# Two weight sums per block pair, and the residual additions of two down-projection parts, moved from VectorE to GpSimd

## The chip, the cores and the metric

The program runs on one core of a Trainium2 chip. The core has a matrix engine (PE, TensorE), two elementwise engines that matter here (DVE, VectorE, and ACT, ScalarE), a programmable engine (POOL, GpSimd) and a queue engine (SP, SyncE) that issues DMA transfers. Each engine takes its instructions strictly in the order in which the built program lists them, and engines wait for one another by semaphores. POOL issues DMA transfers too: those that add into what already lies in on-chip memory (accumulating DMAs). The metric is the device time of one execution in microseconds (us); lower is better.

## The reference

The model is a trunk of two layers on 512 tokens of width 1024 in float32. Each layer mixes tokens by three gated branches, multiplies the merged result by `w_o` and adds it to `x`, then does a gated feed-forward step (the part that is changed), then a gated per-layer embedding:

```python
x = x + merged @ w_o[i]
h = rmsnorm(x, norm_ffn[i])
x = x + (jax.nn.silu(h @ w_ffn_gate[i]) * (h @ w_ffn_up[i])) @ w_ffn_down[i]
h = rmsnorm(x, norm_ple[i])
x = x + jax.nn.sigmoid(h @ w_ple_gate[i]) * (p[i] @ w_ple_in[i])
```

The feed-forward width is 2816, that is 22 blocks of 128.

## The kernel before, in words

Activations are held transposed: 8 chunks of 128 features by 512 tokens, `x[0]` to `x[7]`. A float32 operand is split into a high part in the matrix engine's reduced type (ACT, line 147) and the rest, the low part (DVE, line 161), and a product is three matrix products: high by high, high by low, low by high.

**The output projection** (`w_o`, L930) makes one chunk m at a time: its weights are loaded by SP (L175) and split, PE multiplies, DVE adds the result to the old `x[m]` (loaded by SP at L938), and ACT and DVE split the scaled sum into the halves `wo_h`. `quarters` (L958) makes, after every second chunk, four sums of halves of tokens and chunks (`wo_t`) and splits them (`wo_rp`, `wo_v`, `wo_b`, `wo_z`); the feed-forward step multiplies by these.

**The feed-forward step** (`ffn`, L1100) goes over three parts of 8, 7 and 7 pairs; a pair, counted 0 to 21 here, is gate block `fb` with up block `fb`. `seven` (L989) computes a pair by seven products in place of eight (a two by two scheme over gate and up, halves of the weights' rows, and halves of the tokens). For that it needs four sums of weight halves. The first two, s1 and s2, are made by DMA: SP loads a half (L999, L1000), POOL issues a DMA that adds another half onto it (L1004). The third and fourth are `s3 = s1 + a22` and `s4 = s3 + g[:, up]`, where `a22` is a separate load (tile `ffn_r`, L1002) and `g` holds the gate weights (tile `ffn_wr`, L1001). All of `g`, `a22`, (s1, s2) and (s3, s4) are then split by ACT and DVE; the split of (s3, s4) goes to the tiles `ffn_pt` for even pairs and `ffn_y` for odd ones.

The sums lie in four wide slots: three that rotate for (s1, s2) and a single one for (s3, s4), so the third sum of a pair can only be written once the split of the pair before has read the slot. `ffn_qk_4772` names the tile of the first two slots in layer one, `ffn_qk_4773` that of the third slot and of (s3, s4). There are two buffers of `ffn_r` and three of `ffn_wr`, which the weights of `w_o` and of the down projection share.

After each part, 8 chunks of the down projection are made (L1121 to L1129): PE multiplies, DVE scales the result by the row factor into `ffn_t`, and adds it onto `x[m]`. After the third part the sum is also scaled and split for the next step.

**What sets the order.** PE's instructions stand as written, which the program asks for explicitly. Those of the other engines are put in order by a scheduler that works through them by priority, its own estimate of their lengths, and their dependencies; the weight work of `seven` has a raised priority (L993). `behind` (L1081) adds an order that is not a dependency: in the kernel before it holds s3 of a pair behind the low part of `a22`, and, for all of the first part and the first pairs of the others, behind a marked point of the work ahead (`self.mark` is the low half of chunk 4 in `w_o`).

Of the kernel before, what the change touches and what calls it, by code (L numbers as in the profile page):

```python
# [12 lines left out]
F32R = mybir.dt.float32r  # L13
I32 = mybir.dt.int32
AF = mybir.ActivationFunctionType
ALU = mybir.AluOpType
# [4 lines left out]
P = 128  # L21
# [18 lines left out]
PARTS = (range(0, 8), range(8, 15), range(15, 22))  # L40
# [25 lines left out]
class Net:  # L66
# [922 lines left out]
    def seven(self, wg, wu, bs, tags, spare, md, first, fb):  # L989


        nc = self.nc
        with self.tc.high_priority(offset=min(self.w_ahead, self.tc.cur_priority - self.p0)):  # L993
            lo, up = slice(0, 512), slice(512, 1024)
            g, a22 = self.sb("wr", [P, 1024]), self.sb("r", [P, 512])
            sums = self.sums[self.sevens % 3], self.sums[3]
            self.sevens += 1
            s1, s2, s3, s4 = (s[:, q:q + 512] for s in sums for q in (0, 512))
            nc.sync.dma_start(s1, wg[:, lo])  # L999
            nc.sync.dma_start(s2, wu[:, up])  # L1000
            nc.sync.dma_start(g, wg)  # L1001
            nc.sync.dma_start(a22, wu[:, up])  # L1002
            for q in (s1, s2):
                nc.gpsimd.dma_start(q, wu[:, lo], accum_op=ALU.add)  # L1004
            ws = {}

            def halve(hi, lo, src, names):
                i = self.split(hi, lo, src)
                for q, name in enumerate(names):
                    c = slice(q * 512, q * 512 + 512)  # L1010
                    ws[name] = (hi[:, c], lo[:, c])
                return i

            wide = lambda: (self.sb("wh", [P, 1024], F32R), self.sb("wl", [P, 1024], F32R))
            i = halve(*wide(), g, ("a11", "a12"))
            if fb == 1:
                self.behind(i, self.held)
            low = halve(self.sb("kh", [P, 512], F32R), self.sb("a", [P, 512], F32R), a22, ("a22",))
            halve(*wide(), sums[0], ("s1", "s2"))
            i = self.tt(s3, s1, a22, ALU.add)  # L1020
            self.behind(i, low)
            if first or fb < 3:
                self.behind(i, self.held if fb else self.mark)
            self.tt(s4, s3, g[:, up], ALU.add)
            halve(*spare, sums[1], ("s3", "s4"))
        A, C, Q = (self.ps(t, (P, 2, 256)) for t in tags)

        def product(out, w, b, first):
            wh, wl = ws[w]
            mm = nc.tensor.matmul  # L1030
            for k in range(4):
                c = slice(k * P, k * P + P)
                bh, bl = bs[k][b]
                mm(out, wh[:, c], bh, start=first and k == 0, stop=False, skip_group_check=True)  # L1034
                mm(out, wh[:, c], bl, start=False, stop=False, skip_group_check=True)  # L1035
                mm(out, wl[:, c], bh, start=False, stop=k == 3, skip_group_check=True)  # L1036
            self.chunk2()

        o = self.sb("t", [P, 2, 256])
        p1, p4 = o[:, 0], o[:, 1]  # L1040
        p5 = self.sb("a", [P, 256])
        gg, uu = self.sb("t", [P, 2, 256]), self.sb("t", [P, 2, 256])
        head = fb == 0
        product(A[:, 0], "a11", "b11", True)
        self.act(p1, A[:, 0], AF.Copy)
        if head:
            product(Q[:, 1], "a12", "b21", True)
            product(C[:, 0], "s4", "b22", True)
        product(Q[:, 0], "a22", "t4", True)
        self.act(p4, Q[:, 0], AF.Copy)  # L1050
        five = C[:, int(head)]
        product(five, "s2", "t1", True)
        self.flush(self.act(p5, five, AF.Copy))
        if not head:
            product(A[:, 0], "a12", "b21", False)
        product(Q[:, 0], "s1", "t3", False)
        product(A[:, 1], "s3", "t2", True)
        if head:
            self.tt(gg[:, 0], Q[:, 1], p1, ALU.add)
            self.tt(gg[:, 1], C[:, 0], p5, ALU.add)  # L1060
        else:
            product(C[:, 0], "s4", "b22", False)
        rb = self.rb.rearrange("p (a b) -> p a b", a=2)
        self.tt(p5, p4, p5, ALU.subtract)
        self.tt(gg[:, 0], gg[:, 0] if head else A[:, 0], rb[:, 0], ALU.mult)
        self.tt(p1, A[:, 1], p1, ALU.subtract)
        self.tt(uu[:, 0], p1, Q[:, 0], ALU.subtract)
        self.tt(uu[:, 1], uu[:, 0], p5, ALU.add)
        self.tt(gg[:, 1], gg[:, 1] if head else C[:, 0], p1, ALU.subtract)
        self.tt(gg[:, 1], gg[:, 1], rb[:, 1], ALU.mult)  # L1070

        def rest(then):
            i = self.act(gg, gg, AF.Silu, table="silu")
            if then is not None:
                self.behind(i, then)
            self.tt(gg, gg, uu, ALU.mult)
            self.held = self.split(*self.halves(md), gg.rearrange("p a b -> p (a b)"))

        self.pending.append(rest)
# [19 lines left out]

    def ffn(self, h, x):  # L1100
        self.phase = "ffn"
        i = self.i
        self.halfs, self.pending = 0, []
        st, hn, bs = [], [], self.four
        spare = [[self.sb(t, [P, 1024], F32R) for _ in range(2)] for t in ("pt", "y")]
        md8 = [self.sb(t, [P, 2, 512], F32R) for t in ["v"] * 3 + ["z"] + ["y"] * 3]
        md8.append(tuple(self.sb("e", [P, 512], F32R) for _ in range(2)))
        self.sums, self.sevens = [t for _ in range(2) for t in self.parts_of("qk", [1024], 2)], 0
        for part in PARTS:
            mids = []  # L1110
            for f, fb in enumerate(part):
                tags = (("mm", "mm", "mm"), ("sc", "sc", "av"))[fb % 2]
                md = md8[f]
                mids.append(md)
                wg, wu = self.a["w_fg"][i, fb], self.a["w_fu"][i, fb]
                self.seven(wg, wu, bs, tags, spare[fb % 2], md, part[0] and f < 2, fb)
            self.flush()
            down = [self.a["w_fd"][i, m][:, part[0] * P:(part[-1] + 1) * P] for m in range(KD)]
            two = [self.ps(("mm", "sc")[fb % 2 == 0]) for _ in range(2)]
            self.pair(two, down[:2], mids)  # L1120
            for m in range(KD):  # L1121
                if m < 2:
                    ps = two[m]
                else:
                    ps = self.ps("mm")
                    self.gemm(ps, down[m], mids)
                d = self.sb("t", [P, 512])
                self.tt(d, ps, self.rb, ALU.mult)
                self.tt(x[m], x[m], d, ALU.add)  # L1129
                if part is PARTS[-1]:  # L1130
                    if m in (0, 2):
                        qk = self.parts_of("qk", [2, 512], 2, F32R)
                    hn.append(self.norm_chunk(m, x[m], self.par(i, "ple", m),
                                              qk[m % 2] if m < 4 else "z", st))
        self.main_norm(st[0])
        return hn
# [347 lines left out]
```

## Time and profile before

| What | Value |
|---|---|
| median of 2 runs | 1769.13 us (1768.71 to 1769.55) |
| span of the profiled execution, first to last instruction | 1766.6 us |
| median less span | 2.5 us |
| PE busy | 1759.3 us |
| DVE busy | 1408.6 us |
| ACT busy | 885.5 us |
| POOL busy (DMA issue included) | 98.4 us |

The profiled execution has no separate device time; its span lies 2.5 us below the median of the runs, and sums below are made against the span. Busy time is the union of an engine's instructions; PE's are pipelined and overlap, so that a stream of matrix products counts as busy throughout. The granted clock of PE was 1.000 over the whole span. In layer one, `w_o` runs from about 445 to 489 us and the feed-forward step from 491.6 to about 840 us; in layer two the step begins at 1366.7 us.

### The profile page before, as it was taken

Reading aid. Unit: us, or ns where it says so; the run is one execution under the profiler, and the core shown is the slowest. Engines: PE = TensorE matmul, PEld = TensorE weight load, DVE = VectorE, ACT = ScalarE, POOL = GpSimd, SP = SyncE. Lnnn points to the kernel's source line nnn. Section 1 sums busy time; section 2 is a strip of 40 time slices with the busy share of each in tenths; the row PEclk is TensorE's granted clock in tenths of the full one; section 3 lists DMA queues with packets and bytes.
Section 4 is the critical chain, followed back from the end, with each engine's and each line's share of the span. In section 5 each row is a group of like instructions: output and inputs, shape, how many; then the busy total and the mean of one; then the engine's idle time right before and its main releaser. Section 6 shows DMA issues by size and latency. Waiting matters only on the chain.

```text
span 1766.6 us, 27127 instructions
## 1 busy us (share of the span) xinstructions
PE 1759.3 (100%) x10146; PEld 1551.8 (88%) x10146; DVE 1408.6 (80%) x2354; ACT 885.5 (50%) x1529; POOL 98.4 (6%) x114
## 2 busy tenths in 40 slices
PE   9999999999999999999999999999999999999998
PEld 7888888888899899998888888888888998989987
DVE  7967988998898587787777688889887976867776
ACT  5576555325565254454545655552356643534444
POOL 0000000000111010100000000000001110101000
PEclk9999999999999999999999999999999999999999
DMA  6575641334757365544446655322356674655332
GB/s 231 158 186 160 162 123 54 102 100 150 222 153 196 106 173 156 137 126 127 151 137 173 180 148 154 108 73 94 101 183 194 168 179 118 172 141 156 99 104 96
DMA packets 112548, 253.95 MB, mean 144 GB/s; under 512 B 14368, under 2 KB 23328, under 8 KB 112416
## 3 DMA queue, kind: packets, MB, share of 16 engines
q1 hardware_dynamic: 99024, 227.83, 42.0%
q0 software_dynamic: 12672, 23.07, 8.1%
q8 instruction: 80, 1.31, 0.3%
q10 hardware_dynamic: 720, 1.31, 0.2%
q14 instruction: 52, 0.43, 0.1%
HBM read 214.41 MB, written 7.34 MB: 126 GB/s over the span
## 4 chain that ended last, share of the span: by engine, by line
PE 92%; DVE 4%; DMA 2%; ACT 2%; issue 1%; SPq 0%; POOL 0%; ACTq 0%; POOLq 0%; DVEq 0%
PE ffn_mm L1034 4%; PE ffn_mm L1036 4%; PE ffn_mm L182 4%; PE ffn_mm L181 4%; PE ffn_mm L183 4%; PE ffn_mm L1035 4%; PE ffn_sc L1036 3%; PE ffn_sc L1034 3%; PE ffn_sc L1035 3%; PE mergea_mm L182 2%; PE mergea_mm L183 2%; PE mergea_mm L181 2%; PE gateb_mm L182 2%; PE gateb_mm L183 2%; PE gateb_mm L181 2%; PE wo_mm L182 2%
## 5 line engine op out<-in xcount | busy, mean ns | idle before, releaser
L164 DVE SCALAR_TENSOR_TENSOR conv_z<-glu_z,pre_par,conv_z 128x512 f32<-128x512 f32 x240 | 179.6, 748 | 3.5
L147 ACT ACTIVATE ffn_wh<-ffn_wr 128x1024 fp32r<-128x1024 f32 (+1 forms) x92 | 92.8, 1015 | 111.9 <-PE ffn_mm L182 81.4
L1004 POOL DMA_DIRECT2D ffn_qk<-w_fu x88 | 78.1, 978 | 605.6 <-DMA ffn_qk<-w_fu 289.7
L161 DVE TENSOR_TENSOR ffn_wl<-ffn_wr,ffn_wh 128x1024 fp32r<-128x1024 f32 (+1 forms) x92 | 107.4, 1173 | 5.3 <-ACT ffn_wh L147 4.6
L161 DVE TENSOR_TENSOR ffn_t<-ffn_mm,wo_rb 128x512 f32<-128x512 f32 (+1 forms) x64 | 38.7, 605 | 68.4 <-PE ffn_mm L183 68.4
L147 ACT ACTIVATE mergea_wh<-mergea_wr 128x1024 fp32r<-128x1024 f32 (+1 forms) x32 | 27.1, 848 | 96.8 <-PE mergea_mm L182 79.5
L147 ACT ACTIVATE ffn_wh<-ffn_qk 128x1024 fp32r<-128x1024 f32 x44 | 46.7, 1061 | 37.1 <-PE ffn_mm L182 15.9
L161 DVE TENSOR_TENSOR ffn_wl<-ffn_qk,ffn_wh 128x1024 fp32r<-128x1024 f32 x44 | 53.9, 1224 | 10.7 <-ACT ffn_wh L147 10.7
L161 DVE TENSOR_TENSOR ffn_t<-ffn_t,ffn_t 128x512 f32<-128x512 f32 (+1 forms) x46 | 31.3, 680 | 31.9 <-ACT ffn_t L147 31.4
L147 ACT ACTIVATE natten_e<-natten_e,natten_s 128x192 f32<-128x192 f32 (+1 forms) x88 | 39.3, 474 | 25.2 <-DVE natten_s L726 21.9
L181 PE MATMUL ffn_mm<-ffn_v,ffn_wh 128*128 128x512 f32 x132 | 51.4, 389 | 0.0
L182 PE MATMUL ffn_mm<-ffn_v,ffn_wh 128*128 128x512 f32 x132 | 51.4, 389 | 0.0
L183 PE MATMUL ffn_mm<-ffn_v,ffn_wl 128*128 128x512 f32 x132 | 51.3, 389 | 0.0
L181 PE MATMUL ffn_mm<-ffn_y,ffn_wh 128*128 128x512 f32 x132 | 51.3, 389 | 0.0
L182 PE MATMUL ffn_mm<-ffn_y,ffn_wh 128*128 128x512 f32 x132 | 51.3, 389 | 0.0
L183 PE MATMUL ffn_mm<-ffn_y,ffn_wl 128*128 128x512 f32 x132 | 51.3, 389 | 0.0
L147 ACT ACTIVATE diff_a<-diff_sc,diff_s 128x512 f32<-128x512 f32 x32 | 22.0, 687 | 57.1 <-DVE diff_s L919 57.0
L1036 PE MATMUL ffn_mm<-wo_h,ffn_wl 128*128 128x256 f32 x176 | 49.8, 283 | 0.0
L1036 PE MATMUL ffn_sc<-wo_h,ffn_wl 128*128 128x256 f32 x176 | 49.8, 283 | 0.0
L1035 PE MATMUL ffn_sc<-wo_h,ffn_wh 128*128 128x256 f32 x176 | 49.8, 283 | 0.0
L1035 PE MATMUL ffn_mm<-wo_h,ffn_wh 128*128 128x256 f32 x176 | 49.8, 283 | 0.0
L1034 PE MATMUL ffn_sc<-wo_h,ffn_wh 128*128 128x256 f32 x176 | 49.8, 283 | 0.0
(879 smaller groups left out, 6539.8 us busy)
## 6 DMA issues: line engine op xcount, KB each, us to landing
ffn_qk<-w_fu POOLq DMA_DIRECT2D x88, 256.0 KB, 5.7
ffn_wr<-w_fg SPq DMA_DIRECT2D x44, 512.0 KB, 3.7
ffn_wr<-w_fd SPq DMA_DIRECT2D x32, 448.0 KB, 4.1
ffn_r<-w_fu SPq DMA_DIRECT2D x44, 256.0 KB, 4.2
ffn_qk<-w_fg SPq DMA_DIRECT2D x44, 256.0 KB, 4.0
ffn_qk<-w_fu SPq DMA_DIRECT2D x44, 256.0 KB, 4.2
natten_wr<-w_in SPq DMA_DIRECT2D x16, 512.0 KB, 4.3
diff_wr<-w_in SPq DMA_DIRECT2D x16, 512.0 KB, 4.2
```

The costliest lines, as they stand in the source:

```text
L147: i = self.nc.scalar.activation(out, in_, func, **kw)
L161: return self.nc.vector.tensor_tensor(out, a, b, op)
L164: return self.nc.vector.scalar_tensor_tensor(out, a, s, b, op0, op1)
L181: mm(out, wh, ah, start=first, stop=False)
L182: mm(out, wh, al, start=False, stop=False)
L183: mm(out, wl, ah, start=False, stop=last)
L1004: nc.gpsimd.dma_start(q, wu[:, lo], accum_op=ALU.add)
L1034: mm(out, wh[:, c], bh, start=first and k == 0, stop=False, skip_group_check=True)
L1035: mm(out, wh[:, c], bl, start=False, stop=False, skip_group_check=True)
L1036: mm(out, wl[:, c], bh, start=False, stop=k == 3, skip_group_check=True)
```

## The change

The additions that make s3 and s4 (L1018 and L1022 before, L1020 and L1021 after), 44 of each in the program, go to GpSimd. With them go both order rules on s3: nothing holds it back now but its data and its slot. The addition onto `x[m]` (L1129 before, L1127 after) goes to GpSimd for the first two parts, 32 in all; the third part's 16 stay on VectorE. What is computed stays the same.

```diff
@@ seven
-            low = halve(self.sb("kh", [P, 512], F32R), self.sb("a", [P, 512], F32R), a22, ("a22",))
+            halve(self.sb("kh", [P, 512], F32R), self.sb("a", [P, 512], F32R), a22, ("a22",))
             halve(*wide(), sums[0], ("s1", "s2"))
-            i = self.tt(s3, s1, a22, ALU.add)
-            self.behind(i, low)
-            if first or fb < 3:
-                self.behind(i, self.held if fb else self.mark)
-            self.tt(s4, s3, g[:, up], ALU.add)
+            nc.gpsimd.tensor_tensor(s3, s1, a22, ALU.add)
+            nc.gpsimd.tensor_tensor(s4, s3, g[:, up], ALU.add)
             halve(*spare, sums[1], ("s3", "s4"))
@@ ffn
                 self.tt(d, ps, self.rb, ALU.mult)
-                self.tt(x[m], x[m], d, ALU.add)
+                add = nc.vector if part is PARTS[-1] else nc.gpsimd
+                add.tensor_tensor(x[m], x[m], d, ALU.add)
                 if part is PARTS[-1]:
```

PE's list is the same but for line numbers. Three places where the other lists changed follow; layer two has the same moves.

POOL, from the last normalisation ahead of the feed-forward step to pair 2 (rows of `L1004` are the accumulating DMAs: `4772` twice for pair 0, twice for pair 1, and `4773` twice for pair 2; `ffn_r_4775` and `ffn_wr_4774` belong to pair 0, `4920` and `4919` to pair 1, `5049` and `5048` to pair 2):

```order
 L227 TENSOR_TENSOR conv_rc_4005<-conv_sm_4003,pre_power_104 128x4
-L1004 DMA ffn_qk_4772<-w_fu 128x512 x4
+L1004 DMA ffn_qk_4772<-w_fu 128x512 x2
+L1020 TENSOR_TENSOR ffn_qk_4773<-ffn_qk_4772,ffn_r_4775 128x512
+L1004 DMA ffn_qk_4772<-w_fu 128x512 x2
 L1004 DMA ffn_qk_4773<-w_fu 128x512 x2
+L1021 TENSOR_TENSOR ffn_qk_4773<-ffn_qk_4773,ffn_wr_4774 128x512
+L1020 TENSOR_TENSOR ffn_qk_4773<-ffn_qk_4772,ffn_r_4920 128x512
+L1021 TENSOR_TENSOR ffn_qk_4773<-ffn_qk_4773,ffn_wr_4919 128x512
+L1020 TENSOR_TENSOR ffn_qk_4773<-ffn_qk_4773,ffn_r_5049 128x512
+L1021 TENSOR_TENSOR ffn_qk_4773<-ffn_qk_4773,ffn_wr_5048 128x512
```

The four accumulating DMAs of pairs 1 and 2 now stand behind s3 of pair 0, and s4 of pair 0 behind them.

SP, in the middle of `w_o` (`wo_x_4523` and `wo_x_4624` are the old values of chunks 4 to 7; `ffn_r_5049` is `a22` of pair 2, whose buffer is that of pair 0):

```order
 L999 DMA ffn_qk_4773<-w_fg 128x512
 L1000 DMA ffn_qk_4773<-w_fu 128x512
+L1002 DMA ffn_r_5049<-w_fu 128x512
 L938 DMA wo_x_4523<-xT 128x512 x2
 L938 DMA wo_x_4624<-xT 128x512 x2
```

The load of `a22` of pair 2, which stood some ten transfers later, now stands ahead of four loads of `w_o`; it waits for s3 of pair 0 to have read the buffer.

DVE, at the same place (`wo_wl_4629` is the low part of the weights of chunk 6, `wo_h_4517` that of the activations of chunk 3, `ffn_pt_4760` that of (s3, s4) of pair 0):

```order
 L161 TENSOR_TENSOR wo_x_4423<-wo_x_4423,wo_mm_4485 128x512
 L161 TENSOR_TENSOR wo_wl_4629<-wo_wr_4627,wo_wh_4628 128x1024
+L161 TENSOR_TENSOR ffn_pt_4760<-ffn_qk_4773,ffn_pt_4759 128x1024
 L164 SCALAR_TENSOR_TENSOR wo_h_4517<-wo_x_4423,pre_par_67,wo_h_4517 128x512
 L161 TENSOR_TENSOR wo_ss_4413<-wo_ss_4413,wo_t_4520 128x512
```

The low part of (s3, s4) of pair 0 stood two chunks later, behind the low part of chunk 4; ACT's high part of it moved by as much. From then on the split of (s3, s4) stands about one pair earlier in both lists than before; that of pair 1 (`ffn_y`) now stands inside `w_o`, ahead of the low half of chunk 6.

More of the change, by code (lines that the diff above doesn't have):

```diff
@@ L1101, in ffn @@
         self.phase = "ffn"
-        i = self.i
+        i, nc = self.i, self.nc
         self.halfs, self.pending = 0, []
```

## The prediction, made before the changed kernel had run

> **What bounds the kernel now.** I read the page's busy times first, then what PE waited for, then stretches of the feed-forward step, and then the single rows of the one place where the new order ties two queues together.
>
> ```profile
> span 1766.6 us, 27127 instructions
> ...
> PE 1759.3 (100%) x10146; PEld 1551.8 (88%) x10146; DVE 1408.6 (80%) x2354; ACT 885.5 (50%) x1529; POOL 98.4 (6%) x114
> ```
>
> PE fills the span but for 1766.6 − 1759.3 = 7.3 us. The chain of waits of PE has two rows in all:
>
> ```profile
> PE pre_av L329 <- DVE pre_zeror L402: 1.1, 1, 1.1
> PE natten_av L763 <- DVE natten_a L161: 0.3, 1, 0.3
> ```
>
> Neither stands in the feed-forward step. So PE waits nowhere for the additions that move, and a relieved DVE has nothing to hand on: a gain above 7.3 us (0.4%) is excluded as long as PE does the same products. The question is only whether the change makes PE wait. The next view gives stretches; its columns are span, PE, weight loads, DVE, ACT and POOL busy (with counts), PE's clock, the DMA share and GB/s.
>
> ```profile
> 532.63:542.67 10.04, 10.04 (x86) 10.04 (x85) 9.02 (x16) 5.68 (x9) 1.77 (x2) 1.00 0.74 203
> 572.79:616.34 43.55, 43.55 (x194) 36.05 (x193) 23.06 (x32) 9.69 (x11) 0.00 (x0) 1.00 0.36 116
> 476.70:496.90 20.20, 20.20 (x112) 17.63 (x111) 18.76 (x41) 16.80 (x31) 2.34 (x3) 1.00 0.46 124
> 440.00:475.00 35.00, 35.00 (x156) 29.00 (x155) 26.14 (x39) 19.40 (x29) 5.50 (x6) 1.00 0.85 255
> 1310.00:1345.00 35.00, 35.00 (x156) 29.00 (x155) 27.85 (x43) 18.91 (x29) 5.31 (x6) 1.00 0.92 282
> ```
>
> One steady pair takes PE 10.04 us, in which DVE is busy 9.02 (first row). In the down projection DVE is busy 23.06 of 43.55 (second row). The tightest place is the third row, the end of `w_o`: DVE is busy 18.76 of 20.20, and ACT 16.80.
>
> **What leaves DVE.**
>
> ```profile
> L161 DVE TENSOR_TENSOR ffn_qk<-ffn_qk,ffn_r x44: 683/685/689, 475.5 to 1653.9; 128x512 f32<-128x512 f32 x44
> L161 DVE TENSOR_TENSOR ffn_qk<-ffn_qk,ffn_wr x44: 680/685/693, 476.7 to 1656.0; 128x512 f32<-128x512 f32 x44
> L161 DVE TENSOR_TENSOR wo_x<-wo_x,ffn_t x48: 682/686/693, 586.8 to 1709.1; 128x512 f32<-128x512 f32 x48
> ```
>
> 88 sums and 32 of the 48 additions onto `x`, 120 × 0.685 = 82 us of busy time (some 72 with the overlap of neighbours, 0.61 from start to start). None of it lies on PE's path, so it is worth 0. In a steady pair DVE falls from 9.02 to 9.02 − 2 × 0.60 = 7.82.
>
> **What arrives on GpSimd.** The trace shows no two-input 128x512 operation there. The nearest rows:
>
> ```profile
> masks.py:199 POOL TENSOR_SCALAR_AFFINE_SELECT pre_ident<-pre_ident 128x128 f32<-128x128 f32 x1 | 0.3, 294 | 0.1
> masks.py:197 POOL MEMSET pre_ident<- 128x128 f32 x1 | 0.2, 205 | 0.3 <-POOLq L1473 0.3
> ```
>
> Wait for the ends first. Below: no row shows GpSimd quicker per element than DVE, so not under DVE's 0.69. In the middle: the one-input row, 294 ns for 128 elements, is 4 × 0.294 = 1.18 for 512. Above: two inputs as two such passes, 2.35. I take T = 1.2, the one-input row's rate, since a second input read beside the first costs little on DVE either. Both ends are kept.
>
> Whether the two engines also hinder each other is shown, weakly, by a small operation of GpSimd:
>
> ```profile
> 307.53 1.43 POOL L227 TENSOR_TENSOR diff_rc<-diff_sm,pre_power 128x4 f32<-128x4 f32 x1 [29.30 <-PE branchc_mm L182]
> ...
> 410.96 1.01 POOL L227 TENSOR_TENSOR conv_rc<-conv_sm,pre_power 128x4 f32<-128x4 f32 x1 [102.00 <-PE pin_sc L182]
> ```
>
> ```profile
> 307.35 0.75 DVE L164 SCALAR_TENSOR_TENSOR conv_z<-glu_z,pre_par,conv_z 128x512 f32<-128x512 f32 x1
> ```
>
> The same form takes 1.01 us in one place and 1.43 where it starts inside a DVE instruction with two operands from on-chip memory; 307.35 + 0.75 = 308.10 is 0.57 after its start, about the 0.42 that it lost. So an addition may hold DVE up for between 0 and T. With the whole T, a steady pair costs DVE 7.82 + 2 × 1.2 = 10.2 us against PE's 10.04: 0.2 over per pair, 1.6 in a part of 8. The cover is the lead of the split sums:
>
> ```profile
> 529.51 1.23 DVE L161 TENSOR_TENSOR ffn_wl<-ffn_qk,ffn_wh 128x1024 fp32r<-128x1024 f32 x1 [0.18 <-ACT ffn_wh L147]
> ```
>
> ```profile
> 535.50 0.28 PE L1034 MATMUL ffn_mm<-wo_rp,ffn_wh 128*128 128x256 f32 x1
> ```
>
> They are ready at 530.74 and used at 535.50, a lead of 4.8 us. 1.6 fits inside, and the down projection gives the lag back. So the steady pairs cost **0** at T = 1.2.
>
> The Trainium skill, page "SBUF — State Buffer", section "SBUF: two separate sides", speaks against the change: DVE and GpSimd share a port pair as an exclusive lock, which a DVE operation with two SBUF inputs and a GpSimd operation that reads SBUF take from each other for a whole instruction. The 1.43 against 1.01 agrees; by that rule the hindrance is the full T, which is the second rival below, and at T = 1.2 it would put the handover at its upper bound, 5.9 per layer, and the time at 1781. The Trainium skill, page "GPSIMD Engine Reference", section "3.1 Elementwise — side-by-side cycle accounting", has 4497 ns for an add of 2048 elements; a quarter of it, 1.12 us, is an estimate for this one, and by it the sum would come out the same.
>
> The additions onto `x`: DVE is half idle there (23.06 of 43.55), POOL does nothing (0.00), and `x[m]` is read next a whole part later. **0**. If that cover failed, the next pairs' third sums would be late behind them in POOL's list, by at most the few additions ahead of them, some us per part; the lead of 4.8 us takes most of that.
>
> **Where the new order waits.** At the handover from `w_o` three lists are tied together. In time order, first POOL and the transfers (names, kind, count, KB each, median us to landing), then SP:
>
> ```profile
> 449.27 1.06 POOL L1004 DMA_DIRECT2D ffn_qk<-w_fu  x1 [37.30 <-DVE gatec_x L161]
> ```
>
> ```profile
> wo_wr<-w_o SPq DMA_DIRECT2D x3, 512.0 KB, 7.2
> ffn_qk<-w_fu POOLq DMA_DIRECT2D x6, 256.0 KB, 7.9
> wo_x<-xT SPq DMA_DIRECT2D x4, 256.0 KB, 10.3
> ffn_wr<-w_fg SPq DMA_DIRECT2D x2, 512.0 KB, 4.9
> ```
>
> ```profile
> 449.84 2.39 SPq L938 DMA_DIRECT2D wo_x<-xT  x4
> 458.32 1.46 SPq L175 DMA_DIRECT2D wo_wr<-w_o  x2
> 464.08 11.21 SPq L1001 DMA_DIRECT2D ffn_wr<-w_fg  x3
> ```
>
> s3 of pair 0 waits for the accumulating transfer issued at 449.27: 449.27 + 7.9 = 457.2, done at 458.4. Queued behind it on POOL are the accumulating transfers of pairs 1 and 2, about 7 us later than now but used only from some 500 us on. SP's load of `a22` of pair 2 waits for that s3, and behind it stand the four `wo_x` loads: 449.84 becomes 458.4, 8.6 later. They land by 458.4 + 2.4 + 10.3 = 471.1; the first is wanted at 472.79:
>
> ```profile
> 469.65 0.75 DVE L164 SCALAR_TENSOR_TENSOR wo_h<-wo_x,pre_par,wo_h 128x512 fp32r<-128x512 f32 x1
> ...
> 472.79 0.69 DVE L161 TENSOR_TENSOR wo_x<-wo_x,wo_mm 128x512 f32<-128x512 f32 x1 [1.79 <-PE wo_mm L183]
> ...
> 476.11 0.69 DVE L161 TENSOR_TENSOR wo_ss<-wo_ss,wo_t 128x512 f32<-128x512 f32 x1
> 476.72 0.69 DVE L161 TENSOR_TENSOR ffn_qk<-ffn_qk,ffn_wr 128x512 f32<-128x512 f32 x1
> ...
> 478.92 1.22 DVE L161 TENSOR_TENSOR ffn_pt<-ffn_qk,ffn_pt 128x1024 fp32r<-128x1024 f32 x1
> ...
> 484.13 0.69 DVE L161 TENSOR_TENSOR wo_x<-wo_x,wo_mm 128x512 f32<-128x512 f32 x1
> ...
> 496.18 0.76 DVE L161 TENSOR_TENSOR wo_z<-wo_t,wo_z 128x256 fp32r<-128x256 f32 x2
> ```
>
> That is hidden with 1.7 us to spare. The weights of `w_o` behind them (458.32) go some 3 us later and land by 469 to 470; PE takes them from here, so they are hidden as well:
>
> ```profile
> 478.03 0.39 PE L181 MATMUL wo_mm<-mergeb_y,wo_wh 128*128 128x512 f32 x1
> ```
>
> s4 of pair 0 waits for the gate weights, 464.08 + 4.9 = 469.0 in today's traffic; I add 2.5, since the `wo_x` loads now crowd into those microseconds: 471.5, and s4 ends at 472.7. Then comes ACT's high part:
>
> ```profile
> L147 ACT ACTIVATE ffn_pt<-ffn_qk x22: 1042/1046/1066, 477.4 to 1647.2; 128x1024 fp32r<-128x1024 f32 x22
> ```
>
> and DVE's low part (1.22), which ends at about 475.2 with the hops. But DVE's list has this low part ahead of `wo_h` of chunk 3, which ran at 469.65. So six instructions of `w_o`, done between 469.65 and 476.72, wait behind it: twice 0.75, three times 0.69 and 1.22, less 0.08 of overlap each (476.11 to 476.72 is 0.61), 4.3 us. They end at 479.5 instead of 476.72. From 476.72 to the addition at 484.13 DVE had no gap: 7.41, less the moved s4 (0.61) and low part (1.22), is 5.6, so that addition starts at 485.1, a lag of 1.0. The low part of pair 1's sums, too, now stands inside `w_o`: +1.2, lag 2.2. DVE's 20.20 − 18.76 = 1.44 us of idle time could take some of it; most of that idle time waits on results of ACT, which slip as well, so I take 0.5: lag 1.7. Last, s3 and s4 of pairs 1 and 2 run beside this stretch, each holding DVE for 0 to T; I take half, 0.6 × 4 = 2.4: lag 4.1. The cover is here:
>
> ```profile
> 497.55 0.28 PE L1035 MATMUL ffn_mm<-wo_z,ffn_kh 128*128 128x256 f32 x1
> ```
>
> The last low part of `wo_z` ends at 496.94 and PE wants it at 497.55: 0.6. **PE stalls 3.5 us per layer**, with bounds of 1.1 (no hindrance) and 5.9 (the whole T each); and 0 if s4 is early enough. Layer two has the same order, and more DMA and DVE load (0.92 and 27.85 against 0.85 and 26.14), so it is counted alike: 7.0 in all.
>
> **Sum.** 1766.6 + 7.0 = 1773.6 for the span; the median of the runs lies 2.5 above the span, so 1776.
>
> **Rivals.** *The cover holds, no slower.* If the gate weights land at 469.0 and ACT's high part slips in at once, the low part ends at 472.6; the 1.79 us in which DVE idles for PE at 472.79 swallow the rest of the delay, and DVE carries 1.2 us less from s3 and s4. Then nothing is late: 1768 to 1771. For it speaks that PE never waits here now; against it, that DVE has 1.44 us of freedom where two more low parts and four hindrances come in.
>
> *DVE fills up through the hindrance, slower.* The place is the steady pairs. When an addition holds DVE for its whole T, the pair needs 7.82 + 2T against 10.04. Over T = 1.11 the lag grows by 2T − 2.22 per pair; from T = 1.41 a part of 8 pairs eats its 4.8 us of lead and PE waits. With 22 pairs in three parts, a layer then loses 22 × (2T − 2.22) − 3 × 4.8: at T = 1.6, 7.2 us, for both layers 14, and with the handover about 1790. Over 2% takes T = 1.76 (14.2 per layer, 28 in all, 1804); at T = 2.35 it is 80 us and 1856. For it speak the 1.43 and DVE's 9.02 of 10.04; against it the one-input rate, and that a GpSimd addition which falls into one of DVE's gaps, or beside an operand from the accumulators, costs less than T.
>
> *Faster* needs PE's 7.3 idle us, which lie elsewhere. That the additions stay where they were is excluded by the order of the built program.
>
> **How the numbers follow.** Handover stall (1771 to 1783): 0.50. Cover holds (1768 to 1771): 0.25. DVE full (1783 and up): 0.22, of it 0.08 over 1804. Slightly faster (1760 to 1768): 0.03. About 2% is what a measurement of this kernel can tell from no change; so over 2% faster 0.01, within 0.91, slower 0.08. The range 1768 to 1800 takes in the first two cases and the third up to T = 1.73, and leaves out some 0.12.
>
> **What would show it.** In the changed profile: an addition on POOL of about 1.2 us; PE's waits with a row of some 3 us in each layer at the first quarter sums (`wo_z`, near 497); DVE idle ahead of `ffn_pt` near 470; DVE instructions that grow longer beside POOL's; steady pairs still at 10.04. I am wrong if steady pairs are longer than 10.04 (T too small), if PE waits in `w_o` itself for the late `wo_x` loads, or if no wait appears at 497.

## The result, and the profile after

The changed kernel takes 1785.36 us (median of 2 runs, 1785.34 to 1785.38) against 1769.13 before: a ratio of 1.0092, 95% interval 1.0063 to 1.0121. It is 16.2 us slower, where 7 were forecast. The time lies in the range, and the whole loss was made at the place that the forecast named, but it was more than twice as large.

The page of the profile after, its span and its busy times:

```profile
span 1783.6 us, 27281 instructions
...
PE 1764.2 (99%) x10146; PEld 1555.2 (87%) x10146; DVE 1437.7 (81%) x2234; ACT 891.7 (50%) x1529; POOL 279.0 (16%) x234
```

The span grew by 17.0 us (the median lies 1.8 us above it here, 2.5 before). DVE has 120 instructions fewer, which took 82 us, and is still busy 29 us longer (1437.7 against 1408.6): what stayed on it was stretched by some 111 us, 0.9 for each of the 120 additions. That is the first sign that GpSimd holds it up. PE's waits (what it waited for, us in total, times, longest):

```profile
PE ffn_mm L1031 <- ACT wo_h L147: 5.9, 2, 3.0
PE ffn_mm L1032 <- DVE wo_h L164: 5.5, 4, 1.6
...
PE wo_mm L183 <- DVE wo_wl L161: 0.8, 1, 0.8
```

All three rows are new and stand at the handovers from `w_o` to the feed-forward step, at 494 to 501 us and at 1367 to 1385. They name `wo_h`, the split activations of chunks 6 and 7, and `wo_wl`, the low part of weights of `w_o`; none names the quarter sums `wo_z`. The stretches of the changed kernel (columns as in the prediction) show the handover in layer one, a moment of that in layer two, a steady pair and the first down projection:

```profile
476.70:496.90 20.20, 17.96 (x89) 14.94 (x87) 19.09 (x31) 15.39 (x25) 6.74 (x3) 1.00 0.25 79
495.00:500.00 5.00, 1.32 (x8) 0.82 (x6) 5.00 (x10) 4.90 (x10) 4.92 (x4) 0.71 0.00 2
500.00:505.00 5.00, 4.13 (x23) 4.13 (x24) 4.86 (x13) 3.93 (x9) 2.11 (x3) 0.61 0.83 158
...
1380.00:1385.00 5.00, 0.79 (x2) 0.50 (x3) 5.00 (x8) 4.30 (x8) 4.83 (x4) 0.61 0.07 11
```

```profile
540.00:550.04 10.04, 10.04 (x87) 10.04 (x85) 10.01 (x14) 5.62 (x10) 4.44 (x4) 1.00 0.72 176
...
583.00:627.00 44.00, 44.00 (x206) 36.87 (x205) 24.02 (x21) 12.06 (x13) 20.08 (x15) 1.00 0.29 93
```

In steady pairs PE has no gap, though DVE is now busy 10.01 of 10.04 us where it was 9.02: the engine that was to be relieved is full. In the down projection DVE is no less busy than before, and PE has no gap either. Everything is lost in the first table: PE works 1.32 of 5.00 us, and its granted clock falls to a mean of 0.71 and 0.61.

How long the additions take on GpSimd:

```profile
L1020 POOL TENSOR_TENSOR ffn_qk<-ffn_qk,ffn_r x44: 1287/1655/4329, 457.1 to 1660.7; 128x512 f32<-128x512 f32 x44
L1021 POOL TENSOR_TENSOR ffn_qk<-ffn_qk,ffn_wr x44: 1277/1370/2161, 475.4 to 1662.2; 128x512 f32<-128x512 f32 x44
L1127 POOL TENSOR_TENSOR wo_x<-wo_x,ffn_t x32: 1282/1295/2278, 592.1 to 1620.3; 128x512 f32<-128x512 f32 x32
```

The shortest, 1.28 us, is taken as the addition by itself (T; the prediction took 1.2); the rest is read as waiting for DVE.

The handover row by row. SP, POOL, ACT and DVE of the changed kernel:

```profile
458.38 0.33 SPq L1002 DMA_DIRECT2D ffn_r<-w_fu  x1
458.76 2.31 SPq L938 DMA_DIRECT2D wo_x<-xT  x4
461.16 1.11 SPq L175 DMA_DIRECT2D wo_wr<-w_o  x2
464.27 25.45 SPq L1001 DMA_DIRECT2D ffn_wr<-w_fg  x4
```

```profile
475.40 1.28 POOL L1021 TENSOR_TENSOR ffn_qk<-ffn_qk,ffn_wr 128x512 f32<-128x512 f32 x1 [10.38 <-DMA ffn_wr<-w_fg]
479.11 1.74 POOL L1020 TENSOR_TENSOR ffn_qk<-ffn_qk,ffn_r 128x512 f32<-128x512 f32 x1 [2.43 <-DVE ffn_pt L161]
480.92 1.63 POOL L1021 TENSOR_TENSOR ffn_qk<-ffn_qk,ffn_wr 128x512 f32<-128x512 f32 x1
493.52 4.33 POOL L1020 TENSOR_TENSOR ffn_qk<-ffn_qk,ffn_r 128x512 f32<-128x512 f32 x1 [10.97 <-DVE ffn_y L161]
```

```profile
471.38 1.06 ACT L147 ACTIVATE wo_wh<-wo_wr 128x1024 fp32r<-128x1024 f32 x1 [3.76 <-DMA wo_wr<-w_o]
476.71 1.06 ACT L147 ACTIVATE ffn_pt<-ffn_qk 128x1024 fp32r<-128x1024 f32 x1 [4.26 <-POOL ffn_qk L1021]
477.68 0.71 ACT L147 ACTIVATE wo_h<-wo_x,pre_par 128x512 fp32r<-128x512 f32 x1
```

```profile
477.81 1.23 DVE L161 TENSOR_TENSOR ffn_pt<-ffn_qk,ffn_pt 128x1024 fp32r<-128x1024 f32 x1 [4.10 <-ACT ffn_pt L147]
478.95 0.75 DVE L164 SCALAR_TENSOR_TENSOR wo_h<-wo_x,pre_par,wo_h 128x512 fp32r<-128x512 f32 x1
479.61 1.78 DVE L161 TENSOR_TENSOR wo_ss<-wo_ss,wo_t 128x512 f32<-128x512 f32 x1
...
481.92 1.72 DVE L161 TENSOR_TENSOR wo_wl<-wo_wr,wo_wh 128x1024 fp32r<-128x1024 f32 x1
...
497.25 2.30 DVE L161 TENSOR_TENSOR wo_z<-wo_t,wo_z 128x256 fp32r<-128x256 f32 x2
...
503.73 0.75 DVE L161 TENSOR_TENSOR wo_z<-wo_t,wo_z 128x256 fp32r<-128x256 f32 x2
```

SP's `ffn_r` is held until 458.38, and the four `wo_x` and two `w_o` loads behind it go out together, right ahead of the gate weights. These are issued at the same time as before (464.27, 464.08), but s4 can only start at 475.40. ACT stands idle for 4.26 us in front of the high part, DVE for 4.10 in front of the low part. Then the sums of pairs 1 and 2 hold DVE: 1.78 in place of 0.69, 1.72 in place of 1.22, 2.30 in place of 0.76, together 3.1 us. The last `wo_z` ends at 504.48 instead of 496.94. What PE waits for comes a little sooner in that list, the low part of chunk 7. Before, and the instruction of PE that takes it:

```profile
491.88 0.75 DVE L164 SCALAR_TENSOR_TENSOR wo_h<-wo_x,pre_par,wo_h 128x512 fp32r<-128x512 f32 x1
```

```profile
494.26 0.28 PE L1035 MATMUL ffn_mm<-wo_h,ffn_wh 128*128 128x256 f32 x1
```

After:

```profile
500.07 0.74 DVE L164 SCALAR_TENSOR_TENSOR wo_h<-wo_x,pre_par,wo_h 128x512 fp32r<-128x512 f32 x1
```

It ends at 500.81 instead of 492.63, 8.2 us later, where 1.6 us were to spare.

### The profile page after: what moved, and what is told of

Read it like the earlier page. It is cut to its first block, busy times and chain, and to the rows that moved or that the text cites. A ratio compares the mean times of both kernels' runs of the same rounds, so it can differ in the third digit from the quotient of the medians.

```text
span 1783.6 us, 27281 instructions
## 1 busy us (share of the span) xinstructions
PE 1764.2 (99%) x10146; PEld 1555.2 (87%) x10146; DVE 1437.7 (81%) x2234; ACT 891.7 (50%) x1529; POOL 279.0 (16%) x234
## 4 chain that ended last, share of the span: by engine, by line
PE 91%; DVE 5%; DMA 2%; ACT 1%; issue 1%; POOL 0%; POOLq 0%; ACTq 0%; DVEq 0%; SPq 0%
PE ffn_mm L182 4%; PE ffn_mm L181 4%; PE ffn_mm L183 4%; PE ffn_mm L1032 4%; PE ffn_mm L1031 4%; PE ffn_mm L1033 4%; PE ffn_sc L1033 3%; PE ffn_sc L1031 3%; PE ffn_sc L1032 3%; PE mergea_mm L183 2%; PE mergea_mm L182 2%; PE mergea_mm L181 2%; PE diff_sc L828 2%; PE diff_mm L181 2%; PE diff_mm L183 2%; PE diff_mm L182 2%
## 5 line engine op out<-in xcount | busy, mean ns | idle before, releaser
L161 DVE TENSOR_TENSOR ffn_wl<-ffn_wr,ffn_wh 128x1024 fp32r<-128x1024 f32 (+1 forms) x92 | 123.9, 1352 | 8.5 <-ACT ffn_wh L147 7.9
L1004 POOL DMA_DIRECT2D ffn_qk<-w_fu x88 | 78.6, 978 | 294.9 <-DVE ffn_t L161 138.7
L227 POOL TENSOR_TENSOR diff_rc<-diff_sm,pre_power 128x4 f32<-128x4 f32 x8 | 8.9, 1118 | 563.0 <-DVE diff_sm L164 504.4
L1020 POOL TENSOR_TENSOR ffn_qk<-ffn_qk,ffn_r 128x512 f32<-128x512 f32 x44 | 78.1, 1774 | 60.4 <-DVE ffn_y L161 26.7
L1021 POOL TENSOR_TENSOR ffn_qk<-ffn_qk,ffn_wr 128x512 f32<-128x512 f32 x44 | 68.1, 1548 | 41.6 <-DMA ffn_wr<-w_fg 38.6
L1127 POOL TENSOR_TENSOR wo_x<-wo_x,ffn_t 128x512 f32<-128x512 f32 x32 | 49.0, 1537 | 72.5 <-DVE ffn_t L161 72.5
L161 DVE TENSOR_TENSOR ffn_a<-ffn_r,ffn_kh 128x512 fp32r<-128x512 f32 x44 | 57.4, 1305 | 0.0
L1031 PE MATMUL ffn_mm<-wo_h,ffn_wh 128*128 128x256 f32 x176 | 50.4, 286 | 5.9 <-ACT wo_h L147 5.9
L1032 PE MATMUL ffn_mm<-wo_h,ffn_wh 128*128 128x256 f32 x176 | 50.6, 288 | 5.5 <-DVE wo_h L164 5.5
L147 ACT ACTIVATE ffn_t<-ffn_t 128x512 f32<-128x512 f32 x44 | 27.7, 629 | 47.3 <-DVE ffn_t L161 47.3
```

The lines of the kernel that those rows point to most:

```text
L147: i = self.nc.scalar.activation(out, in_, func, **kw)
L161: return self.nc.vector.tensor_tensor(out, a, b, op)
L1020: nc.gpsimd.tensor_tensor(s3, s1, a22, ALU.add)
L1021: nc.gpsimd.tensor_tensor(s4, s3, g[:, up], ALU.add)
```

## The experiments

The kernel before was run beside each group of runs, at medians of 1768.8 to 1769.3 us; ratios are against those.

**Which part of the change.** First the sums alone (in the changed kernel):

```diff
-                add = nc.vector if part is PARTS[-1] else nc.gpsimd
-                add.tensor_tensor(x[m], x[m], d, ALU.add)
+                self.tt(x[m], x[m], d, ALU.add)
```

> The changed kernel with the additions onto x back on VectorE; the third and fourth sums stay on GpSimd. Theory (all the loss is made at the two handovers from w_o to the feed-forward step, by the sums of the first pairs): 1785, within 1 us of the changed kernel. Rival (part of the loss is DVE held up by the additions onto x in the down projections): 1778 or less.

Measured: 1785.36 us, ratio 1.0093 (1.0078 to 1.0108), the changed kernel's time. Then the additions onto x alone (in the kernel before):

```diff
-                self.tt(x[m], x[m], d, ALU.add)
+                add = nc.vector if part is PARTS[-1] else nc.gpsimd
+                add.tensor_tensor(x[m], x[m], d, ALU.add)
```

> The kernel before with only the additions onto x of the first two parts on GpSimd. Theory: 1769, no PE wait more than before, although each addition holds DVE for about 1 us, since DVE is half idle there. Rival: 1775 or more.

Measured: 1768.91 us, ratio 1.000 (0.999 to 1.0009). The down projection of that kernel, over the same stretch that the prediction quotes of before:

```profile
572.79:616.34 43.55, 43.55 (x195) 36.10 (x194) 24.27 (x25) 10.01 (x11) 11.82 (x7) 1.00 0.34 107
```

DVE issues seven instructions fewer there and is busy 24.27 us instead of 23.06: the additions that left cost DVE more than they saved, and it does not matter, since half of DVE's time is free. The whole loss is the sums'.

**Whether it is only the first pairs.** The sums of the first three pairs back on VectorE, with their rules (cut: `low` is the low part of `a22`):

```diff
+            if fb < 3:
+                i = self.tt(s3, s1, a22, ALU.add)
+                self.behind(i, low)
+                self.behind(i, self.held if fb else self.mark)
+                self.tt(s4, s3, g[:, up], ALU.add)
+            else:
                 nc.gpsimd.tensor_tensor(s3, s1, a22, ALU.add)
                 nc.gpsimd.tensor_tensor(s4, s3, g[:, up], ALU.add)
```

> The changed kernel with s3 and s4 of the first three pairs of each layer back on VectorE, with the two order rules that they had; the other 38 of each and the additions onto x stay on GpSimd. Theory (handover): 1769 to 1771, PE's waits at the first quarter sums gone, DVE still near 10.0 of 10.04 us in the steady pairs. Rival (DVE full in the steady pairs costs PE time too): 1776 or more.

Measured: 1782.23 us, ratio 1.0069 (1.0054 to 1.0084). The theory in this form fell. The waits at the end of `w_o` are gone, but a new one stands at 531 us and at 1411; the waits of PE and the row of ACT in front of it in this kernel:

```profile
PE ffn_sc L1037 <- ACT ffn_t L147: 8.0, 2, 4.7
```

```profile
528.97 1.06 ACT L147 ACTIVATE ffn_pt<-ffn_qk 128x1024 fp32r<-128x1024 f32 x1 [3.79 <-POOL ffn_qk L1027]
```

It is the same thing one step later: at the pairs where the sums pass to GpSimd, ACT's list has a high part ahead of other work (here the copies of PE's results), and it waits there for a late s4. So the loss goes with the changeover and not with `w_o` alone; only this second place was tried.

**What makes the handover late: SP's list.** One order rule on SP; the lists of the other engines stay the same row for row (cut: `self.load_x` is the load of `wo_x`, the last of them by then):

```diff
-            nc.sync.dma_start(a22, wu[:, up])
+            load = nc.sync.dma_start(a22, wu[:, up])
+            if fb == 2:
+                self.behind(load, self.load_x)
```

> The changed kernel with one order rule more on SP alone: the load of a22 of pair 2 stands behind the last four wo_x loads again, as in the kernel before. Theory A (the late gate weights come from SP's queue, since four wo_x and two w_o loads crowd with them): s4 of the first pair starts at 470 to 471 in place of 475.4, the low part behind it 4 to 5 us sooner, PE stalls some 4 us less per layer: 1775 to 1777. Theory B (the gate weights are late because of the accumulating transfers, which POOL still issues late): s4 at 474 or later and 1783 to 1785.

Measured: 1776.77 us, ratio 1.0049 (1.0032 to 1.0066); 8.6 us of the 16.2 are gone, as theory A said. s4 of pair 0 in this kernel:

```profile
470.67 1.29 POOL L1023 TENSOR_TENSOR ffn_qk<-ffn_qk,ffn_wr 128x512 f32<-128x512 f32 x1 [6.28 <-DMA ffn_wr<-w_fg]
```

4.7 us sooner than in the changed kernel, from one transfer that no longer stands in front of six others.

**What makes the rest: the place of the first split, or the hold.** The low part of pair 0's sums put where it stood before, without SP's rule and with it:

```diff
-            halve(*spare, sums[1], ("s3", "s4"))
+            low = halve(*spare, sums[1], ("s3", "s4"))
+            if fb == 0:
+                self.behind(low, self.mark)
```

> The changed kernel with one rule more: the low part of (s3, s4) of pair 0 stands behind the low part of chunk 4 on VectorE, where it stood before; SP's list stays as changed, so s4 still starts at about 475.4. Theory (what DVE loses is the wait of that low part for a late s4, 4.1 us of idle time in front of it): 4 us less per layer, 1776 to 1779. Rival (ACT's high part of the same sums stands ahead as before and holds ACT until 476.7, and DVE needs ACT): 1782 to 1786.

> The changed kernel with both rules: SP's load of a22 behind the wo_x loads, and the low part of pair 0's sums behind that of chunk 4. Theory (order makes all of the loss, hindrance of DVE by GpSimd is small change): 1769 to 1772. Rival (the four sums of pairs 1 and 2 inside the stretch hold DVE up by 3.2 us per layer by the profile, 1.10 + 0.50 + 1.6, and this is left): 1773 to 1776.

Measured: 1786.71 us, ratio 1.0101 (1.0087 to 1.0115), and with SP's rule 1778.91, ratio 1.0054 (1.004 to 1.0068). Neither gained anything over its partner without the low part's move. VectorE of the second kernel says why:

```profile
473.48 0.75 DVE L164 SCALAR_TENSOR_TENSOR wo_h<-wo_x,pre_par,wo_h 128x512 fp32r<-128x512 f32 x1 [4.46 <-ACT wo_h L147]
```

The low part is out of the way, and VectorE waits 4.46 us all the same, now for ACT, whose high part of the same sums still stands in front of its `wo_h`. So the high part (`self.high`) was moved as well, one row of ACT's list more (cut: `self.mark_high` is ACT's high part of chunk 4):

```diff
+                self.behind(self.high, self.mark_high)
```

> The kernel with SP's rule and the late low part, and one row more moved: ACT's high part of pair 0's (s3, s4) stands behind ACT's high part of chunk 4 of the activations. Theory (in e6 it was ACT's list that held VectorE: VectorE idled 4.46 us for ACT's wo_h, which stood behind that high part; without it the stretch has room for the 3 us of hindrance): VectorE's idle time at 473 gone, PE waits under 1 us per layer, 1769 to 1772. Rival (hindrance alone fills VectorE in this stretch, order has no further part): 1775 to 1779.

Measured: 1772.21 us, ratio 1.0018 (1.0009 to 1.0027). VectorE and PE's waits in this kernel:

```profile
473.69 0.69 DVE L161 TENSOR_TENSOR wo_x<-wo_x,wo_mm 128x512 f32<-128x512 f32 x1 [1.65 <-PE wo_mm L183]
474.61 1.23 DVE L161 TENSOR_TENSOR wo_wl<-wo_wr,wo_wh 128x1024 fp32r<-128x1024 f32 x1 [0.23 <-ACT wo_wh L147]
475.75 0.75 DVE L164 SCALAR_TENSOR_TENSOR wo_h<-wo_x,pre_par,wo_h 128x512 fp32r<-128x512 f32 x1
476.41 1.22 DVE L161 TENSOR_TENSOR ffn_pt<-ffn_qk,ffn_pt 128x1024 fp32r<-128x1024 f32 x1
```

```profile
PE ffn_mm L1037 <- DVE wo_h L164: 2.3, 2, 1.1
```

But for 0.23 us, VectorE idles here only for PE, as in the kernel before (1.65 us; 1.79 then), and PE waits 1.1 us per layer instead of about 6. Then the hold by itself: the sums of pairs 1 and 2 made a quarter as long (the rest of them is left out), with SP's rule and without:

```diff
-            nc.gpsimd.tensor_tensor(s3, s1, a22, ALU.add)
-            nc.gpsimd.tensor_tensor(s4, s3, g[:, up], ALU.add)
+            n = 128 if fb in (1, 2) else 512
+            nc.gpsimd.tensor_tensor(s3[:, :n], s1[:, :n], a22[:, :n], ALU.add)
+            nc.gpsimd.tensor_tensor(s4[:, :n], s3[:, :n], g[:, up][:, :n], ALU.add)
```

> The changed kernel with SP's order rule, and s3 and s4 of pairs 1 and 2 of each layer made over 128 of their 512 columns (three quarters of these two pairs' sums are left out); the lists of all engines are the same row for row. Theory (what is left at the handover with SP's order right is GpSimd holding DVE up for as long as an addition lasts): the hold of 3.2 us per layer falls to about 1, the last wo_z is no longer late, PE waits under 0.5 us per layer: 1769 to 1771. Rival (DVE is late because a whole pair's split stands earlier in its list): 1775 to 1777, as with SP's order alone.

> The same quarter-length sums of pairs 1 and 2 without SP's order rule. Theory (late gate weights and hindrance add up): the hold goes, the 4.1 us of DVE idle time ahead of the first low part stay: 1776 to 1779. Rival (either alone is covered, only both together make the loss): 1770 to 1773.

Measured: 1771.41 us, ratio 1.0014 (1.0005 to 1.0024), and without SP's rule 1778.84, ratio 1.0064 (1.0047 to 1.0081). Shorter additions are worth 5.4 us with SP's list mended and 6.5 without; SP's rule 7.4 with short additions and 8.6 with long ones. The two add up nearly, 14.0 of 16.2 us together. e9 and e12 also show that what SP's rule leaves can be taken away, but for 2 to 3 us, in either of two ways: by shortening the additions, or by putting the first split back to its old place on both engines.

**Whether the dropped order rules are to blame.** The changed kernel with both rules on s3 back, all sums on GpSimd (cut as above). The rule with a mark holds for pairs 0 to 2 and the first two pairs of each later part, as its condition says, and not for all of the first part; in the steady pairs only the rule behind the low part of `a22` acts.

```diff
-            nc.gpsimd.tensor_tensor(s3, s1, a22, ALU.add)
+            i = nc.gpsimd.tensor_tensor(s3, s1, a22, ALU.add)
+            self.behind(i, low)
+            if first or fb < 3:
+                self.behind(i, self.held if fb else self.mark)
```

> The changed kernel with the two order rules on s3 kept as in the kernel before, on the new engine; all the additions stay on GpSimd. Theory (the loss comes from the dropped rules, which let the sums of each pair stand a pair earlier in the lists; the additions themselves cost PE nothing): 1768.5 to 1771, with DVE 9.9 to 10.04 of 10.04 us in the steady pairs. Rival (the move itself costs, by the hindrance of DVE at the handover): 1773 to 1779.

Measured: 1804.75 us, ratio 1.0196 (1.0183 to 1.021): the theory fell, and so did its rival. Stretches of this kernel, the handover and some steady pairs, then PE's waits and a row of VectorE:

```profile
476.70:496.90 20.20, 20.20 (x110) 17.55 (x109) 17.86 (x38) 16.29 (x30) 1.81 (x2) 1.00 0.46 128
...
640.00:690.00 50.00, 47.53 (x381) 46.92 (x380) 37.30 (x53) 22.70 (x37) 19.31 (x17) 0.97 0.63 150
```

```profile
PE ffn_sc L1036 <- DVE ffn_wl L161: 9.1, 11, 0.9
PE ffn_mm L1036 <- DVE ffn_wl L161: 6.6, 7, 0.9
```

```profile
655.31 1.23 DVE L161 TENSOR_TENSOR ffn_y<-ffn_qk,ffn_y 128x1024 fp32r<-128x1024 f32 x1 [4.89 <-ACT ffn_y L147]
```

The handover is free again (20.20 of 20.20), and the steady pairs pay: with the rule each sum comes late, and the low parts of the next weights (`ffn_wl`, for which PE waits) stand on VectorE behind the split of those sums, idle for 4.89 us. VectorE is busy only 37.30 of 50.00 there, so it is not full but queued behind a late result. Set beside the changed kernel, this says that dropping the rules was what put the sums early enough to hide GpSimd's slowness in the steady pairs; the price was paid once per layer at the handover. Two runs on the length of the additions in this kernel, first each made twice (in the cut, the second of each), then all from pair 1 on a quarter as long:

```diff
+            nc.gpsimd.tensor_tensor(s3, s1, a22, ALU.add)
+            nc.gpsimd.tensor_tensor(s4, s3, g[:, up], ALU.add)
```

> As the kernel with the rules kept, but each s3 and each s4 is made twice by GpSimd (the second writes the same numbers again). Theory (each addition holds DVE up for nearly its length alone, 1.28 us): DVE needs 7.8 + 4 x 1.28 = 12.9 us per pair against 10.04, less 4.8 us of lead per part: 49 us per layer, about 1870. Rival (the hindrance is small, and GpSimd itself has room: 1.8 + 4 x 1.3 = 7 of 10.04 us): within 10 us of the kernel with the rules kept.

> The kernel with the order rules kept, but all sums from pair 1 on made over 128 of 512 columns (the rest is left out). The lists stay but for pair after pair a weight split or a load that changes places with its neighbour. Theory (in that kernel PE waits because s3 and s4 take 3.3 us on GpSimd instead of 1.2 on VectorE, start late by the rule, and DVE stands in line behind them): 1769 to 1776. Rival (the lists themselves are bad): 1795 or more.

Measured: 1875.0 us, ratio 1.0596 (1.0576 to 1.0615), and 1770.35 us, ratio 1.0007 (0.9998 to 1.0017). The first hits its expected time by luck: that was worked out from a start of about 1770, and the kernel that it doubles already stands at 1804.75, so the doubling cost 70, not 98. Both of its readings fail in part: it costs much, and VectorE is not saturated (busy 43.05 in the same 50 us):

```profile
640.00:690.00 50.00, 44.11 (x348) 42.88 (x346) 43.05 (x42) 19.52 (x32) 31.72 (x23) 0.97 0.53 128
```

The second shows that the length of the additions is what costs in this order: shortening them returns 34 of the 35 us, though some weight splits changed places with a neighbour too. Whether it is the lateness of the sums or the hold on VectorE that weighs more there was not told apart.

No version beat the kernel before: PE has 7.3 us of idle time to give, and none of it waits for these additions.

## Why the prediction was right or wrong

**What bounds the kernel: right.** PE had nothing to gain, and every us lost is a wait of PE that was not there before, or what follows from it.

**What leaves DVE is worth nothing: right**, and less than nothing for DVE itself: 82 us left, 111 came back as hold.

**T = 1.2: right in kind**, 1.28 measured. With the full hold the prediction had 10.2 us of DVE per steady pair; 10.01 is measured, in a window of 10.04 that it can't exceed, and 10.01 − 7.82 is 2.2 for the two additions, 1.1 each, a little under T. The pairs stayed at 10.04, as the 4.8 us of lead said.

The Trainium skill, page "SBUF — State Buffer", section "SBUF: two separate sides", states an exclusive lock between the two engines. The trace agrees: the `wo_ss` that starts beside GpSimd's addition takes 1.78 us instead of 0.69, 1.09 more, nearly T.

**The additions onto x, 0: right** (e2).

**The handover, the place: right; the size: wrong, 3.5 us per layer against 8.5** (17.0 us of span over two layers), above its own upper bound of 5.9. The terms of the lag that were mis-sized:

- *Gate weights at 471.5.* The prediction added 2.5 us for the `wo_x` loads that come at once; s4 started at 475.40, 3.9 later. e4 shows that it was those loads: with them out of the way s4 starts at 470.67, and PE's loss falls by 4.3 us per layer. "The weights of `w_o` land by 469 to 470" failed with it, for the same reason: ACT had to wait for them to 471.38.
- *Hindrance 2.4 us.* 3.1 by the three stretched rows. A small error.
- *Idle time of DVE, 0.5 us used.* Before, DVE idled 0.76 + 0.39 + 0.19 = 1.3 us between 490 and 494; in the changed kernel it idles 0.1 from 477.81 on. Some 0.8 more was absorbed.

4.1 + 3.9 + 0.7 − 0.8 is 7.9 of lag; the last `wo_z` was 7.5 late.

The last step, from the lag to PE, took the wrong operand. The prediction set the lag against `wo_z`, wanted at 497.55 with 0.6 us to spare. PE waits earlier, for `wo_h`: 8.2 us of lag and 1.6 to spare are 6.6 us. Then *PE's clock* comes in, for which no term was given; it costs about 1.5 us per layer (below). Together 8.1, and PE takes that `wo_z` at 505.64, 8.1 us later than before and no longer waiting for it. Layer two loses 8.9. There PE also waits 0.8 us inside `w_o`, for a low part of its weights, which the prediction called hidden.

One link was misread without harm to the sum: the prediction let VectorE's list do the blocking, and passed over ACT's, in which the high part stands just as early. e5 and e6 moved the low part alone and gained nothing; e12 moved both and did.

**The rivals.** The cover did not hold. DVE did fill up in the steady pairs, to 10.01 of 10.04, but PE did not wait there; the measured time falls in the band that was given to that rival (1783 and up) for a reason that belongs to the forecast. So it is luck that the range held: it reached above 1783 only to take in part of this rival. e7 does lose in the steady pairs, but not by this rival either, since VectorE is busy only 37.30 of 50.00 us there. (By the prediction's own formula the range ends at T = 1.71, not 1.73; nothing hangs on it.)

## What to carry to other kernels

An operation moved to a slower engine takes its place in three lists, not one: that of the engine, those of the engines that wait for its result in order, and those of the queues that refill what it reads. Look for the first instruction that now stands behind it in each, and for what stands behind that; here a load that waited for the moved sum held up six transfers that had nothing to do with it. And a relief of VectorE by GpSimd is to be counted with the hold: here it came out negative, and only lead and free time elsewhere hid it.

## What the runs showed of the hardware that was not expected

**A short wait slows PE beyond the wait.** PE of the changed kernel after its 2.97 us wait (start, length, instruction):

```profile
498.71 0.58 PE L1031 MATMUL ffn_mm<-wo_h,ffn_wh 128*128 128x256 f32 x1 [2.97 <-ACT wo_h L147]
500.87 0.58 PE L1032 MATMUL ffn_mm<-wo_h,ffn_wh 128*128 128x256 f32 x1 [1.57 <-DVE wo_h L164]
...
502.74 0.41 PE L1033 MATMUL ffn_mm<-wo_h,ffn_pt 128*128 128x256 f32 x1
502.95 0.41 PE L1031 MATMUL ffn_mm<-wo_h,ffn_pt 128*128 128x256 f32 x1
```

```profile
497.10:503.80 6.70, 3.52 (x14) 3.22 (x15) 6.56 (x14) 5.89 (x12) 3.84 (x4) 0.50 0.45 68
```

The granted clock is 0.50 from 497.1 to 503.8. The instructions start 0.21 us apart until then and 0.12 again from 504.1; the excess over 0.12 from 498.7 on, the waits left out, sums to about 1.5 us per layer. With SP's rule (e4) the longest wait is 1.81 us, and in layer one the clock falls still; in layer two, after a wait of the same 1.81 us, it stays at 1.00 (second row):

```profile
495.00:500.00 5.00, 3.81 (x20) 3.81 (x21) 4.86 (x13) 4.18 (x10) 2.11 (x3) 0.69 0.76 118
...
1375.00:1380.00 5.00, 4.70 (x37) 4.50 (x38) 4.86 (x13) 4.25 (x10) 1.44 (x2) 1.00 0.89 172
```

Nor does it fall in layer one of e3, where the wait is 3.35 us:

```profile
531.38 0.38 PE L1037 MATMUL ffn_sc<-wo_h,ffn_wh 128*128 128x256 f32 x1 [3.35 <-ACT ffn_t L147]
```

```profile
530.00:535.00 5.00, 3.62 (x30) 3.62 (x31) 4.95 (x7) 2.09 (x7) 3.67 (x3) 1.00 0.86 196
```

In e12, with 1.1 us, the clock stays at 1.00 over its span. So the length of the wait alone does not decide; what does was not tried. The Trainium skill, page "TensorE: Matmul & The Clock Gate", section "HAM oscillation — how this bites in real kernels", puts the limit at idle gaps of about 3.4 us; here a wait of 1.81 was enough in one place, and the measurement decides.

**GpSimd can be kept out for long.** The s3 that starts at 493.52 takes 4.33 us, 3.0 more than by itself, in both layers, while VectorE runs one instruction after the other at its normal pace. In e9 the same s3 over 128 columns takes nearly as long:

```profile
488.87 3.52 POOL L1023 TENSOR_TENSOR ffn_qk<-ffn_qk,ffn_r 128x128 f32<-128x128 f32 x1 [11.31 <-DVE ffn_y L161]
```

The next addition over 128 columns takes 0.46 there. So most of that time is waiting, and it reads as waiting for VectorE. Elsewhere (479.11, 1.74) an addition came in after a single instruction of VectorE. What decides between the two was not tried.
